# 21 of 44 gate and up tile pairs by seven block products instead of eight

## The chip, the cores and the metric

The kernel runs on one core of a Trainium2 chip. The metric is the time of one execution on the device in microseconds; the kernel before has a median of 1558.62 over 3 runs (1556.32 to 1564.79). The engines are TensorE (PE, products, with its weight loads shown apart as PEld), VectorE (DVE), ScalarE (ACT), GpSimd (POOL) and SyncE (SP, which here only issues DMAs).

## The reference

Two layers on x of 512 positions by 1024. Each layer normalises and modulates x, runs a retention branch and a causal pooling branch, merges them with sigmoid gates, projects, and adds the result to x. Then it normalises again to h2 and runs the feed-forward network (FFN):

```python
mod = c_act @ w_ada[l] + b_ada[l]
sh1, sc1, g1, sh2, sc2, g2 = jnp.split(mod, N_MOD, axis=-1)
...
h2 = modulate(rmsnorm(x, norm2[l]), sh2, sc2)
gate, up = jnp.split(h2 @ w_ffn_in[l], 2, axis=-1)
x = x + g2[:, None, :] * ((jax.nn.silu(gate) * up) @ w_ffn_out[l])
```

`w_ffn_in` is 1024 x 5632, so gate and up have 2816 columns each: 22 tiles of 128. The two layers have 44 pairs of a gate tile and the up tile of the same columns. All data are float32.

## The kernel before

Activations lie transposed: 128 channels on the partitions, 512 positions along a row. To keep float32 accuracy, both operands of a product are split in a high part, rounded to the type that TensorE multiplies fast, and a low part, the rest. `mm3` then makes three products: high weights by high activations, low by high, high by low. `project` runs `mm3` over all 128-channel blocks of the input into one PSUM bank of 128 x 512; there are eight banks (`ps`). An FFN tile has 8 blocks, so 24 products, and a pair 48.

Weights are packed in the order of use into chunks of eight 128 x 128 blocks (`wst`, 512 KB each). `prep` (L464) loads a chunk into a `raw` tile (SP's queue), casts it to `whi` and makes `wlo`: from chunk 16 on ACT writes minus `whi` into `wlo`, and a DMA issued by POOL adds the chunk from memory to it. `unit` (L483) calls `prep` for the chunk in use and, by `LOOK`, for the two behind it. There are 4 `raw` tiles and 5 each of `whi` and `wlo`.

The modulation vector is made on DVE: `mod_tile` (L531) loads a tile of `wada` (512 KB) into a `raw` tile too, and multiplies and sums it with the conditioning vector. `background` hands these out along the program: one per step of the gate loop behind retention, two per step of the pool loop, one per pair in the first FFN half and two in the second. Every `raw` tile, of `wst` or `wada`, is given out in the order in which it is asked for.

The FFN of a layer has two halves of 11 pairs. `first_tiles` (L615) makes the first three tiles, half a row (256 positions) at a time, while the second half of h2 is still being made. Behind each half `close` (L628) multiplies by `w_ffn_out` and adds to x.

The program is recorded first, and `Recorder.order` (L247) then sets the order of each engine by a list of costs: it follows time, gives each engine the operation that can start first or is due first, and lets some operations go to either of two engines (`either`: DVE or POOL; `copy`: ACT or DVE). Buffers of a kind are handed out in order of first use, except for temporaries and rows. PE's own order is that of the program. The engines then run their lists in order, held only by semaphores. As all operations are issued from one line, L390 in the profile is the line of every one of them.

## Time and profile before

| | us |
|---|---|
| median of 3 runs | 1558.62 |
| profiled execution | 1558.66 |
| its span, first to last instruction | 1556.9 |
| PE busy (x7302) | 1525.8 |
| ACT busy (x979) | 777.9 |
| DVE busy (x1133) | 642.7 |
| POOL busy (x331) | 299.8 |
| mean DMA rate | 212 GB/s |

The page shows busy time per engine over the span. A product's busy time overlaps with the next one's, so the pace of products is read from how many start in a stretch, not from the mean of one. A window row of a stretch has its length, the busy time (and instructions) of PE, PEld, DVE, ACT and POOL, the granted clock, the share of the DMA engines' time and the rate in GB/s. Layer 0's FFN runs from about 424 to 788 us (its first products of 256 columns with h2, its last with `w_ffn_out`), layer 1's from about 1182 to 1546.

### The profile page before, as it was taken

Reading aid. Unit: us, or ns where it says so; the run is one execution under the profiler, and the core shown is the slowest. Engines: PE = TensorE matmul, PEld = TensorE weight load, DVE = VectorE, ACT = ScalarE, POOL = GpSimd, SP = SyncE. Lnnn points to the kernel's source line nnn. Section 1 sums busy time; section 2 is a strip of 40 time slices with the busy share of each in tenths; the row PEclk is TensorE's granted clock in tenths of the full one; section 3 lists DMA queues with packets and bytes.
Section 4 is the critical chain, followed back from the end, with each engine's and each line's share of the span. In section 5 each row is a group of like instructions: output and inputs, shape, how many; then the busy total and the mean of one; then the engine's idle time right before and its main releaser. Section 6 shows DMA issues by size and latency. Waiting matters only on the chain.

```text
span 1556.9 us, 18913 instructions
## 1 busy us (share of the span) xinstructions
PE 1525.8 (98%) x7302; PEld 1272.8 (82%) x7302; DVE 642.7 (41%) x1133; ACT 777.9 (50%) x979; POOL 299.8 (19%) x331
## 2 busy tenths in 40 slices
PE   7899999999999999999999999999999999999997
PEld 6688878788988888888897888888889888888887
DVE  8977681245453212233265647314346111011123
ACT  3376664444554433444377777445346443344442
POOL 3212241111111111311111212211111111111110
PEclk9999999999999999999999999999999999999999
DMA  7766859999789999999789686999997998988972
GB/s 256 249 195 150 220 132 237 250 253 290 182 224 256 250 202 240 289 268 269 150 197 233 149 181 144 233 243 261 244 266 165 215 190 191 196 192 191 190 152 77
DMA packets 94589, 329.68 MB, mean 212 GB/s; under 512 B 10529, under 2 KB 12833, under 8 KB 94498
## 3 DMA queue, kind: packets, MB, share of 16 engines
q0 software_dynamic: 35280, 128.47, 47.4%
q1 hardware_dynamic: 59218, 200.00, 37.6%
q8 instruction: 57, 0.93, 0.2%
q14 instruction: 34, 0.28, 0.1%
HBM read 326.32 MB, written 2.10 MB: 211 GB/s over the span
## 4 chain that ended last, share of the span: by engine, by line
PE 91%; DVE 5%; DMA 2%; ACT 1%; issue 1%; POOL 0%; DVEq 0%; SPq 0%; ACTq 0%
PE ps L390 91%; DVE t L390 1%; DVE raw L390 1%; DMA wlo<-wst 1%; DVE mod L390 1%; DMA raw<-wst 1%; DVE r L390 0%; DMA xall<-xT 0%; ACT whi L390 0%; ACT t L390 0%; DVE h L390 0%; ACT r L390 0%; POOL wlo L390 0%; DVE s L390 0%; DVE wlo L390 0%
## 5 line engine op out<-in xcount | busy, mean ns | idle before, releaser
L390 PE MATMUL ps<-h,whi 128*128 128x512 f32 (+1 forms) x2720 | 804.0, 379 | 8.1 <-DVE h L390 5.6
L390 PEld LDWEIGHTS ps<-h,whi 128*128 128x128 f32 x2720 | 499.2, 188 | 111.5 <-issue 4.1
L390 ACT CAST whi<-raw 128x1024 fp32r<-128x1024 f32 (+1 forms) x227 | 238.3, 1050 | 551.7 <-PE ps L390 428.4
L390 PE MATMUL ps<-h,wlo 128*128 128x512 f32 (+1 forms) x1360 | 506.6, 380 | 0.7 <-DMA wlo<-wst 0.7
L390 PE MATMUL ps<-r,whi 128*128 128x512 f32 (+1 forms) x1620 | 440.4, 356 | 3.8 <-DVE r L390 3.8
L390 POOL DMA_DIRECT2D wlo<-wst x245 | 214.1, 874 | 1075.4 <-ACT wlo L390 923.0
L390 PEld LDWEIGHTS ps<-r,whi 128*128 128x128 f32 x1620 | 286.2, 188 | 53.4 <-DVE r L390 7.0
L390 PEld LDWEIGHTS ps<-h,wlo 128*128 128x128 f32 x1360 | 254.9, 188 | 47.4 <-DMA wlo<-wst 0.9
L390 PE MATMUL ps<-r,wlo 128*128 128x512 f32 (+1 forms) x810 | 289.0, 357 | 0.0
L390 ACT ACTIVATE wlo<-whi 128x1024 fp32r<-128x1024 f32 x245 | 259.6, 1061 | 19.0 <-DVE whi L390 11.5
L390 DVE SCALAR_TENSOR_TENSOR raw<-raw,cact 128x1024 f32<-128x1024 f32 x96 | 119.7, 1250 | 335.3 <-DMA raw<-wada 259.3
L390 PEld LDWEIGHTS ps<-r,wlo 128*128 128x128 f32 x810 | 152.2, 188 | 21.4
L390 DVE SCALAR_TENSOR_TENSOR xall<-ps,mod,xall 128x512 f32<-128x512 f32 (+1 forms) x62 | 38.9, 630 | 202.4 <-PE ps L390 202.4
L390 DVE TENSOR_TENSOR t<-ps,t 128x512 f32<-128x512 f32 x60 | 41.3, 689 | 194.8 <-PE ps L390 190.6
L390 PE MATMUL ps<-whi,h 128*128 128x512 f32 x256 | 80.6, 396 | 0.8 <-ACT r L390 0.8
L390 DVE TENSOR_TENSOR r<-t,r 128x512 fp32r<-128x512 f32 (+1 forms) x76 | 54.9, 722 | 9.9 <-ACT r L390 7.4
L390 PEld LDWEIGHTS ps<-whi,h 128*128 128x128 f32 x256 | 48.0, 188 | 12.7 <-ACT r L390 1.2
L390 ACT ACTIVATE t<-ps 128x512 f32<-128x512 f32 x76 | 44.5, 588 | 19.3 <-PE ps L390 19.1
L390 ACT COPY t<-ps 32x512 f32<-32x512 f32 (+1 forms) x72 | 41.5, 579 | 22.5 <-DVE t L390 11.0
L390 ACT ACTIVATE sq<-xall 128x256 f32<-128x256 f32 (+1 forms) x42 | 20.3, 486 | 63.6 <-DVE xall L390 63.3
L390 PE MATMUL ps<-wlo,h 128*128 128x512 f32 x128 | 50.6, 396 | 0.0
L390 ACT CAST r<-t 64x512 fp32r<-64x512 f32 (+1 forms) x60 | 36.9, 618 | 24.8 <-DVE t L390 22.9
(91 smaller groups left out, 868.3 us busy)
## 6 DMA issues: line engine op xcount, KB each, us to landing
raw<-wst SPq DMA_DIRECT2D x261, 512.0 KB, 4.8
wlo<-wst POOLq DMA_DIRECT2D x245, 512.0 KB, 7.1
raw<-wada SPq DMA_DIRECT2D x96, 512.0 KB, 6.5
tab<-rot SPq DMA_DIRECT2D x32, 256.0 KB, 4.8
xall<-xT SPq DMA_DIRECT2D x4, 512.0 KB, 6.5
out<-t SPq DMA_DIRECT2D x7, 256.0 KB, 2.4
out<-t SPq DMA_DIRECT2D x2, 128.0 KB, 2.3
tri<-trid SPq DMA_DIRECT2D x1, 128.0 KB, 5.0
```

The costliest lines, as they stand in the source:

```text
L390: getattr(eng, method)(*[real(a) for a in args], **{k: real(v) for k, v in kw.items()})
```

## The change

21 pairs, the even ones from 4 to 20 in layer 0 and in layer 1 those from 4 to 20 that 3 doesn't divide, are made by `seven`. It takes the 1024 input channels and the two output tiles (gate, up) as a 2 x 2 grid of weight blocks, and h2 as a 2 x 2 grid of channels by positions, each half a row long. A 2 x 2 product of blocks needs eight block products; with sums of blocks on either side (Strassen's method in Winograd's form) seven suffice, and the outputs are sums of the seven. In the code a seven has two chunks, each with the four weight blocks for two of the eight channel blocks: 2 chunks x 7 x 2 x 3 products of 256 columns, where a pair had 48 of 512.

What it adds around the products: `seven_prep` makes four sums of weight blocks per chunk (DVE), splits three of the four blocks themselves (768 columns) and all four sums, and no longer uses the accumulating DMA for them, so a seven's chunk fills four weight tiles, not two. Once per layer `make_h` also writes h2 unsplit (`whole`), and four sums per channel pair are made of it and split. Behind the products one copy (ACT) and five sums (DVE) put gate and up together from four PSUM banks.

SBUF is laid out anew: 3 `raw` tiles for 4; one set of 11 weight tiles `w` for the 10 of `whi` and `wlo`; 8 double tiles `x` for the rotary tables, the scores and `q_low`, and for the sums of h2. The squares go to the temporaries. `background` gives two tiles per step in the gate loop (one before), one per plain pair and per output tile of the first half's `close`, and none at a seven. A change of ACT's function table now counts as part of an operation's cost when the order is made. Two chunks are added for alignment.

```diff
-HALF_FT = FT // 2
+FF_CUTS = (0, 11, FT)
...
-N_CHUNKS = -(-N_UNITS // UNITS)
+N_CHUNKS = -(-N_UNITS // UNITS) + DEPTH
...
-N_RAW, N_SPLIT, N_H, N_ROW, N_TEMP, N_SCORE, N_SQ = 4, 5, 2 * KT, 28, 9, 5, 2
+N_RAW, N_W, N_X, N_H, N_ROW, N_TEMP = 3, 11, 8, 2 * KT, 28, 9
...
+SEVEN = [set(range(4, FT, 2)), {i for i in range(3, FT) if i % 3}]
+HALF_KT = KT // 2
...
                     if e == "scalar" and o.table is not None and o.table != table:
-                        t = max(t, free[e] + TABLE_US)
+                        d += TABLE_US
...
-    def raw_tile(dt=F32):
-        return nc.tile(wp, [P, UNITS * P], dt, "raw", N_RAW)
+    def weights():
+        return nc.tile(wp, [P, UNITS * P], F32R, "w", N_W)
+
+    def raw_tile():
+        return nc.tile(wp, [P, UNITS * P], F32, "raw", N_RAW)
+
+    def pair_tile(dt=F32):
+        return nc.tile(ap, [P, 2, S], dt, "x", N_X)
...
     def prep(c, n=1):
-        if c >= N_CHUNKS or c in his:
+        if c >= N_CHUNKS or c in his or c in sevens:
             return
-        raw = raw_tile()
+        raw, hi, lo = raw_tile(), weights(), weights()
         nc.sync.dma_start(out=raw, in_=wst[c])
-        hi = nc.tile(wp, [P, UNITS * P], F32R, "whi", N_SPLIT)
-        lo = nc.tile(wp, [P, UNITS * P], F32R, "wlo", N_SPLIT)
-        if c >= FIRST_ADDED:
+        if FIRST_ADDED <= c:
 
...
+    sevens = {}
+
+    def seven_chunk(l, i, k0):
+        c = len(order) // UNITS
+        assert len(order) % UNITS == 0
+        for k, col in ((0, 0), (HALF_KT, 0), (HALF_KT, FF), (0, FF)):
+            for d in range(2):
+                order[(l, "ffn_in", k + k0 + d, col + i * P)] = len(order)
+        sevens[c] = None
+        return c
+
+    def seven_prep(c):
+
+        if sevens[c] is not None:
+            return
+        w = 2 * P
+        af = raw_tile()
+        nc.sync.dma_start(out=af, in_=wst[c])
+        ah, al, sh, sl = (weights() for _ in range(4))
+        a11, a12, a22, a21 = (af[:, n * w:n * w + w] for n in range(4))
+        s34, s21 = keep(F32), keep(F32)
+        nc.vector.tensor_sub(out=s34[:, :w], in0=a21, in1=a11)
+        nc.vector.tensor_add(out=s21[:, :w], in0=s34[:, :w], in1=a22)
+        nc.vector.tensor_add(out=s21[:, w:], in0=a21, in1=a22)
+        nc.vector.tensor_sub(out=s34[:, w:], in0=a12, in1=s21[:, :w])
+        copy(ah[:, :3 * w], af[:, :3 * w])
+        if ADD_SEVEN:
+            nc.scalar.activation(al[:, :3 * w], ah[:, :3 * w].bitcast(F32), AF.Copy, scale=-1.0)
+            nc.gpsimd.dma_start(out=al[:, :3 * w], in_=wst[c][:, :3 * w], accum_op=ALU.add)
+        else:
+            nc.either.tensor_sub(out=al[:, :3 * w], in0=af[:, :3 * w], in1=ah[:, :3 * w].bitcast(F32))
+        for n, sf in enumerate((s34, s21)):
+            part = slice(n * S, n * S + S)
+            copy(sh[:, part], sf)
+            nc.either.tensor_sub(out=sl[:, part], in0=sf, in1=sh[:, part].bitcast(F32))
+        sevens[c] = (ah, al), (sh, sl)
...
-        for cc in range(c, c + look[0] + 1):
-            prep(cc)
+        ahead(c)
         sl = slice(o * P, (o + n) * P)
         return his[c][:, sl], los[c][:, sl]
+
+    def ahead(c):
+        for cc in range(c, c + look[0] + 1):
+            if cc in sevens:
+                seven_prep(cc)
+            else:
+                prep(cc)
...
+        if whole is not None:
+            nc.add({
+                "scalar": ("activation", (whole, t, AF.Identity), dict(bias=sh)),
+                "vector": ("tensor_scalar", (), dict(out=whole, in0=t, scalar1=sh, scalar2=None, op0=ALU.add)),
+            })
...
             m_.append(m)
-            background()
+            background(2)
...
+        whole = [(keep(F32), keep(F32)) for _ in range(HALF_KT)]
+        sums = [(pair_tile(F32R), pair_tile(F32R)) for _ in range(HALF_KT)]
...
+        while len(order) % UNITS:
+            order[("none", len(order))] = len(order)
+        done = first_tiles(l, 2, h2, "ffn_in", [0, FF, P], norm_b, block)
+        for k in range(HALF_KT):
+            t13, t24 = temp(), temp()
+            b11, b21, b12, b22 = (block(kk, n) for n, kk in ((0, k), (0, k + HALF_KT), (1, k), (1, k + HALF_KT)))
+            nc.either.tensor_sub(out=t13[:, A], in0=b12, in1=b11)
+            nc.either.tensor_sub(out=t13[:, B], in0=b12, in1=b22)
+            nc.either.tensor_sub(out=t24[:, A], in0=b22, in1=t13[:, A])
+            nc.either.tensor_sub(out=t24[:, B], in0=b21, in1=t24[:, A])
+            hi, lo = sums[k]
+            for n, t in enumerate((t13, t24)):
+                copy(hi[:, n], t)
+                nc.either.tensor_sub(out=lo[:, n], in0=t, in1=hi[:, n].bitcast(F32))
+
+        def seven(i):
+
+            cs = [seven_chunk(l, i, k0) for k0 in (0, 2)]
+            o = [ps() for _ in range(4)]
+            for k in range(HALF_KT):
+                ahead(cs[k // 2])
+                if k % 2:
+                    continue
+                (ah, al), (sh, sl) = sevens[cs[k // 2]]
+
+                for (wh, wl), n, bank, at, act in (
+                    ((ah, al), 0, 0, 0, "b11"), ((ah, al), 1, 1, 0, "b21"), ((ah, al), 2, 3, 1, 3),
+                    ((sh, sl), 2, 1, 1, 2), ((sh, sl), 3, 2, 0, 0), ((sh, sl), 0, 2, 1, 1), ((sh, sl), 1, 3, 0, "b22"),
+                ):
+                    for d in range(2):
+                        ws = slice((2 * n + d) * P, (2 * n + d + 1) * P)
+                        if isinstance(act, str):
+                            a = hs(h2[k + d + HALF_KT * (act[1] == "2")], A if act[2] == "1" else B)
+                        else:
+                            a = tuple(z[:, act // 2, act % 2 * 256:act % 2 * 256 + 256] for z in sums[k + d])
+                        first = k + d == 0 and (bank, at) in ((0, 0), (1, 0), (3, 1), (2, 0))
+                        last = k + d == HALF_KT - 1 and (bank, at) in ((0, 0), (1, 1), (2, 1), (3, 0))
+                        mm3(o[bank][:, at * 256:at * 256 + 256], (wh[:, ws], wl[:, ws]), a, first, last)
+            m1 = temp()[:, A]
+            nc.scalar.copy(out=m1, in_=o[0][:, A])
+            gate, up, u = temp(), temp(), temp()
+            nc.vector.tensor_add(out=gate.halves(), in0=o[1].halves(), in1=m1.twice())
+            nc.vector.tensor_add(out=u.halves(), in0=o[2].halves(), in1=gate[:, B].twice())
+            nc.vector.tensor_add(out=gate[:, B], in0=u[:, A], in1=o[3][:, A])
+            nc.vector.tensor_add(out=up[:, A], in0=u[:, B], in1=o[3][:, B])
+            nc.vector.tensor_add(out=up[:, B], in0=u[:, B], in1=o[2][:, A])
+            nc.scalar.activation(gate, gate, AF.Silu)
+            nc.either.tensor_mul(out=gate, in0=gate, in1=up)
+            return split(gate)
+        for f, (i0, i1) in enumerate(zip(FF_CUTS, FF_CUTS[1:])):
             hid = []
-            for i in range(f * HALF_FT, (f + 1) * HALF_FT):
+            for i in range(i0, i1):
+                if i in SEVEN[l]:
+                    hid.append(seven(i))
+                    continue
                 gu = []
                 for c in (i * P, FF + i * P):
                     if done:
...
                 nc.scalar.activation(sg, gu[0], AF.Silu)
                 nc.vector.tensor_mul(out=sg, in0=gu[1], in1=sg)
                 hid.append(split(sg))
-                background(1 + f)
+                background()
```

In the orders below L390 is the issuing line of the kernel before and L409 that of the changed one; `_` and a number tell buffers apart.

On PE, inside the second FFN half of layer 0: before, the end of one tile and the start of the next (`h` is h2, `whi` and `wlo` the split weights).

```order
L390 MATMUL ps_5515<-h_3667,whi_5383 128x512
L390 MATMUL ps_5515<-h_3667,wlo_5390 128x512
L390 MATMUL ps_5515<-h_3677,whi_5383 128x512
L390 MATMUL ps_5557<-h_3551,whi_5383 128x512
L390 MATMUL ps_5557<-h_3551,wlo_5390 128x512
L390 MATMUL ps_5557<-h_3562,whi_5383 128x512
```

Now, inside a seven (`x` are the sums of h2, `w` the split weights or sums of weights).

```order
L409 MATMUL ps_5853<-h_3589,w_5714 128x256
L409 MATMUL ps_5853<-h_3592,w_5714 128x256
L409 MATMUL ps_5853<-h_3592,w_5722 128x256
L409 MATMUL ps_5853<-h_3605,w_5714 128x256
L409 MATMUL ps_5864<-x_3829,w_5714 128x256
L409 MATMUL ps_5864<-x_3829,w_5722 128x256
L409 MATMUL ps_5864<-x_3840,w_5714 128x256
L409 MATMUL ps_5864<-x_3882,w_5714 128x256
L409 MATMUL ps_5864<-x_3882,w_5722 128x256
L409 MATMUL ps_5864<-x_3915,w_5714 128x256
L409 MATMUL ps_5853<-x_3829,w_5745 128x256
L409 MATMUL ps_5853<-x_3829,w_5751 128x256
```

A tile went into one bank with 512 columns each; now a product takes half a row, the banks alternate within a chunk, and each group of six reads another block of weights.

On DVE, the same part of the program. Before, what one pair asks of it (the product with silu, a split, and two `wada` tiles):

```order
L390 TENSOR_TENSOR t_5403<-ps_5401,t_5403 128x512
L390 CAST r_5447<-t_5403 128x512
L390 TENSOR_TENSOR r_5451<-t_5403,r_5447 128x512
L390 SCALAR_TENSOR_TENSOR raw_5429,mod_0_4216<-raw_5429,cact_73 128x1024
L390 SCALAR_TENSOR_TENSOR raw_5478,mod_0_4216<-raw_5478,cact_73 128x1024
```

Now, from a plain pair to a seven (`raw_6118` is the chunk of a seven, `raw_6049` is read by a cast alone):

```order
L409 CAST w_6148<-raw_6049 128x1024
L409 TENSOR_TENSOR r_6162<-raw_6118 128x256
L409 CAST w_6170<-raw_6118 128x768
L409 TENSOR_TENSOR w_6178<-raw_6118,w_6170 128x768
L409 TENSOR_TENSOR r_6190<-r_6162,raw_6118 128x256
L409 TENSOR_TENSOR r_6190<-raw_6118 128x256
L409 CAST w_6201<-r_6190 128x512
L409 TENSOR_TENSOR w_6207<-r_6190,w_6201 128x512
L409 TENSOR_TENSOR r_6162<-raw_6118,r_6190 128x256
L409 TENSOR_TENSOR t_6217<-ps_6081,t_6154 128x512
L409 TENSOR_TENSOR w_6207<-r_6162,w_6201 128x512
L409 TENSOR_TENSOR w_6229<-raw_6151,w_6209 128x768
```

A chunk that DVE did not touch before now takes up to ten of its instructions in a row. `w_6148`, the cast of `raw_6049`, is read by no product: in the whole program 42 chunks of sevens are first cast, negated and added to in the plain way, with that outcome.

On SP's queue, the loads of about two pairs. Before:

```order
L390 DMA raw_5235<-wst 128x1024
L390 DMA raw_5249<-wada 128x1024
L390 DMA raw_5272<-wada 128x1024
L390 DMA raw_5286<-wst 128x1024
L390 DMA raw_5311<-wst 128x1024
L390 DMA raw_5324<-wada 128x1024
```

Now (`raw_6034` and `raw_6049` are the plain loads of the two chunks that `raw_6118` and `raw_6151` load again; `raw_5992` and `raw_6181` belong to a plain pair):

```order
L409 DMA raw_5992<-wst 128x1024
L409 DMA raw_6034<-wst 128x1024
L409 DMA raw_6049<-wst 128x1024
L409 DMA raw_6085<-wada 128x1024
L409 DMA raw_6118<-wst 128x1024
L409 DMA raw_6151<-wst 128x1024
L409 DMA raw_6181<-wst 128x1024
```

Two chunks and two `wada` tiles per pair became, for a seven and a plain pair together, six loads of chunks and one of `wada`, through three tiles. Over the program there are 305 loads of `wst` on this queue, 261 before, and 247 accumulating loads on POOL's, 245 before.

65 lines of the change are left out of this document (45 added, 20 removed).

## The prediction

> **What bounds the kernel now.** I read the page's engine line and chain of waits first, then the stages, then the pace of single products. The columns of a stage are its length, then busy time and number of instructions of each engine, granted clock, DMA share and rate.
>
> ```profile
> span 1556.9 us, 18913 instructions
> PE 1525.8 (98%) x7302; PEld 1272.8 (82%) x7302; DVE 642.7 (41%) x1133; ACT 777.9 (50%) x979; POOL 299.8 (19%) x331
> ...
> PE 91%; DVE 5%; DMA 2%; ACT 1%; issue 1%; POOL 0%; DVEq 0%; SPq 0%; ACTq 0%
> ```
>
> ```profile
> 0.00:73.00 73.00, 58.38 (x254) 46.42 (x254) 66.04 (x106) 24.00 (x31) 23.48 (x21) 0.95 0.78 254
> ...
> 434.00:600.00 166.00, 166.00 (x757) 137.52 (x756) 44.84 (x77) 73.74 (x78) 26.88 (x31) 1.00 0.94 234
> 600.00:794.00 194.00, 194.00 (x967) 164.31 (x966) 63.05 (x118) 87.08 (x98) 38.57 (x40) 1.00 0.94 242
> ...
> 1154.00:1310.00 156.00, 156.00 (x847) 135.14 (x846) 48.02 (x96) 73.92 (x93) 24.29 (x28) 1.00 0.87 194
> 1310.00:1540.00 230.00, 230.00 (x1076) 191.78 (x1075) 37.42 (x60) 93.23 (x104) 33.79 (x39) 1.00 0.82 171
> ```
>
> The last four rows cover the FFN of the two layers, where the change lies, and some work at its edges. TensorE (PE) is busy in all 746 us of them; the others have room, though the DMA share stands at 0.82 to 0.94. So here a product less is time less, as long as what feeds TensorE stays ahead of it.
>
> **The products.** A plain pair makes 2 tiles x 8 blocks x 3 products of 512 columns: 48. A seven makes 2 x 7 x 2 x 3 = 84 of 256 columns. The pace of each kind, from stretches of one kind alone:
>
> ```profile
> 1310.00:1480.00 170.00, 170.00 (x744) 139.51 (x743) 24.57 (x39) 70.11 (x73) 26.88 (x31) 1.00 0.90 192
> ...
> 400.00:420.00 20.00, 20.00 (x170) 19.95 (x170) 7.47 (x15) 8.78 (x13) 2.56 (x3) 1.00 0.45 98
> ...
> 424.00:439.00 15.00, 15.00 (x125) 14.78 (x124) 14.78 (x37) 9.51 (x19) 0.89 (x1) 1.00 0.58 147
> ```
>
> 170/744 = 0.2285 us for 512 columns; 20/170 = 0.1176 for 256, more than half (0.1142), because there the weight loads (PEld) are 19.95 of 20 us busy: they set the pace. A pair is 48 x 0.2285 = 10.97 us, a seven 84 x 0.1176 = 9.88: 1.09 us gained, x 21 = **22.8 us**, not the eighth (28.8) that the column count gives. The third row shows that pace held (0.12) with the vector engine (DVE) 99% busy, so I charge nothing for the sums' traffic beside the loads.
>
> The Trainium skill speaks against the change here: "TensorE: Matmul & The Clock Gate", section "Back-to-back issue gap", gives about 81 ns for a product of 128 columns and 131 for 512 in a stream of loads and products. An estimate from that page, in a straight line between them, is 98 ns for 256, so 84 x 0.098 = 8.2 against 48 x 0.131 = 6.3: each seven 1.9 us longer, about 41 us in all. The trace has 228 and 118 ns, so the sum goes by the trace; what the page would make of it here is the last rival below.
>
> **What feeds them: a preparation made twice.** Looking ahead from a plain tile, `prep` reaches a seven's chunk before `seven_chunk` has entered it in `sevens`, so it is prepared as a plain chunk too, and nothing reads that. The order shows 42 such chunks: 305 loads of `raw` for 261, and 247 accumulating loads for 245, where 42 should have gone. Each seven still pays 4 plain loads and 2 accumulating ones. The price is in the DMA queues' view, first of the page (packets, MB, share of 16 engines), then of 605 to 720 us (issues, KB, us to landing):
>
> ```profile
> q0 software_dynamic: 35280, 128.47, 47.4%
> q1 hardware_dynamic: 59218, 200.00, 37.6%
> ```
>
> ```profile
> 605.00:720.00 115.00, 115.00 (x505) 94.33 (x504) 38.91 (x68) 48.86 (x51) 26.43 (x26) 1.00 1.01 271
> ...
> raw<-wst SPq DMA_DIRECT2D x22, 512.0 KB, 5.9
> wlo<-wst POOLq DMA_DIRECT2D x21, 512.0 KB, 7.3
> raw<-wada SPq DMA_DIRECT2D x18, 512.0 KB, 7.3
> ```
>
> Layer 0 alternates seven and plain: 20.85 us of TensorE with 7 plain and 4 accumulating loads, 0.336 and 0.192 per us. Layer 1 has two sevens to a plain pair: 30.73 us with 10 and 6, 0.325 and 0.195. The stretch quoted carried 40 and 21 in 115 us, 0.348 and 0.183, with TensorE never idle. So the amount of DMA is known ground.
>
> New is that `raw` has three tiles, not four. A tile's turn is its landing (5.9 us, 7.3 for `wada`) and its reading. Readings, from the groups by shape (after the bar: busy us, mean ns):
>
> ```profile
> L390 ACT CAST whi<-raw 128x1024 fp32r<-128x1024 f32 x226 | 237.7, 1052 | 551.7 <-PE ps L390 428.4 <-DMA raw<-wst 123.2
> ...
> L390 DVE SCALAR_TENSOR_TENSOR raw<-raw,cact 128x1024 f32<-128x1024 f32 x96 | 119.7, 1250 | 335.3 <-DMA raw<-wada 259.3 <-issue 32.3 <-ACT whi L390 31.9
> ...
> L390 DVE TENSOR_TENSOR r<-t,r 128x512 fp32r<-128x512 f32 x60 | 41.5, 692 | 2.0
> ...
> L390 DVE CAST r<-t 128x512 fp32r<-128x512 f32 x64 | 27.5, 430 | 2.2
> ...
> L390 DVE CAST whi<-raw 128x1024 fp32r<-128x1024 f32 x34 | 23.6, 695 | 29.8 <-PE ps L390 25.2 <-DMA raw<-wst 4.0 <-POOL r L390 0.4
> ...
> L390 ACT ACTIVATE h<-t,mod 128x256 fp32r<-128x256 f32 x44 | 21.8, 506 | 15.0 <-DVE t L390 14.9
> ...
> L390 DVE TENSOR_TENSOR acc<-acc,sq 128x256 f32<-128x256 f32 x27 | 11.7, 433 | 11.1 <-ACT sq L390 11.1
> ...
> L390 DVE TENSOR_TENSOR wlo<-raw,whi 128x1024 fp32r<-128x1024 f32 x7 | 8.4, 1223 | 0.7 <-ACT whi L390 0.5
> ```
>
> A seven's chunk is read by four sums of 256 (0.433 each), a cast and a difference of 768 (halfway between the rows of 512 and 1024: 0.56 and 0.96): 3.25 us on DVE. A plain or wasted one is read by a cast (1.05), a `wada` one in 1.25. Layer 0: (6 x 5.9 + 7.3 + 2 x 3.25 + 4 x 1.05 + 1.25)/3 = 18.2 us for a period of 20.85. Layer 1: (10 x 5.9 + 4 x 3.25 + 6 x 1.05)/3 = 26.1 for 30.73. They hold, with 13 to 15% to spare, if a landed tile waits on average no more than 1.1 us (layer 0) or 1.4 us (layer 1) for its reader.
>
> That reader is mostly DVE, which takes its instructions in order. The 32 DVE rows of a period of layer 0's second half, priced by these groups (8 sums and 3 output sums of 256 at 0.433, 10 of 512 at 0.69, 3 casts of 1024, 1 of 768 and 4 of 512, 2 differences of 768, one `wada`), come to 19.2 us of 20.85, 92%; 134 rows over six sevens and three plain pairs of layer 1 come to 78 of 92 us. Before, layer 0's first FFN half gave DVE 45 of 166 us (434 to 600). So DVE becomes nearly as full as TensorE. It also takes 181 casts of whole chunks, not 34, and such a cast waits until TensorE frees a weight tile; behind it stand the output sums that free PSUM banks. A seven holds four of the eight banks, so TensorE has a pair's length, some 10 us, before it waits for those. What that costs is not shown for 350 us on end (9 sevens and 8 pairs, 12 and 5), but two short stretches are like it:
>
> ```profile
> 420.00:434.00 14.00, 13.85 (x110) 13.22 (x109) 13.46 (x35) 9.20 (x18) 1.75 (x2) 1.00 0.92 231
> ...
> 786.00:796.00 10.00, 10.00 (x85) 9.87 (x83) 9.26 (x25) 6.29 (x12) 1.72 (x2) 1.00 1.03 268
> ```
>
> ```profile
> 796.80 0.38 PE L390 MATMUL ps<-h,wlo 128*128 128x256 f32 x1 [0.67 <-DMA wlo<-wst]
> ```
>
> With DVE over 92% and the DMA full, TensorE lost 0.15 us in 420 to 439 and 0.67 right after 796: 0.82 of 30 us, 2.7%. On 350 us that is **9.5 us** lost. The ends are 0 (as in 605 to 720) and the 30 us of the second rival below.
>
> **The rest.** Retention's gate loop now asks for two `wada` tiles per step instead of one, and the pool loop keeps two, on three `raw` tiles. A step of the pool loop has 36 products, 8.23 us, and 1.5 chunks: (1.5 x 6.95 + 2 x 8.55)/3 = 9.2 us for `raw` (6.9 with four). Eight steps of layer 0 would lack 7.6 us, and layer 1 asks for only 11 tiles there; the chunks prepared ahead (11 weight tiles, five chunks of 5.5 us each) cover most. I take **2 us** (0 to 8). The 16 extra whole-precision copies of `h` per layer and the blocks' sums lie under three plain pairs: nothing (16 x 0.5 us on ACT, bare). The start could go either way: DVE loses its stops behind POOL's differences, and the weights' `raw` tile has to land, be cast and be subtracted in a row.
>
> ```profile
> 21.71 2.94 POOL L390 TENSOR_TENSOR wlo<-raw,whi 128x1024 fp32r<-128x1024 f32 x1 [18.06 <-ACT whi L390]
> ```
>
> ```profile
> 22.35 2.31 DVE L390 TENSOR_TENSOR mod<-mod,vec 128x1 f32<-128x1 f32 x1
> ...
> 28.91 2.32 DVE L390 TENSOR_TENSOR mod<-mod,vec 128x1 f32<-128x1 f32 x1
> ```
>
> ```profile
> raw<-wst SPq DMA_DIRECT2D x7, 512.0 KB, 4.4
> ```
>
> A step now takes 6.6 us (28.91 - 22.35), 2.3 of it a one-column sum held up while POOL subtracts; with the difference on DVE (1.22) it would be some 1.1 us shorter. The tile's own chain is 4.4 + 1.05 + 1.22 and a few semaphores, 6.9 us. Seven steps: -7 to +2; I take 0, by the chain.
>
> Sum: the profiled execution took 1558.7 us (span 1556.9 and 1.8 around it; the median is 1558.62, the same). 1558.7 - 22.8 + 9.5 + 2 = **1547 us**.
>
> **Rivals.** *Nothing is lost*: the waits fall into the spare 13%, as in 605 to 720. 1558.7 - 22.8 = 1536. For it: DMA load and pace have both been seen. Against: DVE was a third busy then.
>
> *The raw tiles run dry behind DVE*: a landed tile waits behind an earlier seven's output, 2 sums of 512, 3 of 256, a product and a difference, 4.1 us by their rows, half of that on average: 2 us. Layer 0's period becomes (54.7 + 14)/3 = 22.9, layer 1's (78.3 + 20)/3 = 32.8: 2.05 x 9 + 2.05 x 6 = 30 us lost, 1558.7 - 22.8 + 30 + 2 = 1568, slower. It decides from 1.1 us of waiting on, and each further microsecond costs some 40.
>
> *The DMA engines are the bound*: by the queues' rows an accumulating load takes 0.474 x 1557/245 = 3.0 us of all 16 engines, a plain one (0.524 MB) 0.376 x 1557 x 0.524/200 = 1.53. Layer 0 needs 22.8 of 20.85 us, layer 1 33.4 of 30.73: 17 + 16 us, 1571. Against: 605 to 720 asked for 124 of 115 us and got it. The Trainium skill, "Perfetto Trace Analysis", section "Identifying the Most-Contended Engine", calls the occupancy of the 16 engines misleading; the trace agrees, with a share of 1.00 at 281 GB/s and 1.01 at 271.
>
> ```profile
> 340.00:380.00 40.00, 40.00 (x176) 32.81 (x176) 21.34 (x37) 15.16 (x18) 6.08 (x7) 1.00 1.00 281
> ```
>
> *Loads outgrow the half products*: above 0.1306 us (10.97/84) a seven loses outright; at 0.14, 21 x (11.76 - 10.97) = 17 us, 1575. The 99% stretch speaks against it.
>
> **How the numbers follow.** The forecast has 0.50, nothing lost 0.18, dry tiles 0.22, full DMA 0.05, loads 0.02, the unnamed 0.03. A half per cent, about what can be told apart here, is 7.8 us: 1550.8 to 1566.4. Nothing lost and 0.39 of the forecast lie below, 0.57. The forecast's upper 0.11 and some 0.09 of the dry tiles lie between, 0.20. The rest, 0.23, is slower. The forecast's own range is 1538 to 1560. For 8 in 10 I reach from below the full gain (a start some 3 us better) to beyond the dry tiles: 1533 to 1574.
>
> **What would show it.** In the profile after: 84 products of 256 columns per seven at 0.118 us; TensorE idle in the four FFN stretches of some 10 us in all, in short gaps released by DVE or by a DMA into `w`; DVE at 80 to 90% there; 305 loads of `raw`. Wrong would be: gaps before each seven (dry tiles), a pace over 0.13, or a start or pool loop that moved by more than 8 us.

## The result and the profile after

The changed kernel takes 1632.8 us (median of 4 runs, 1629.0 to 1639.4), the kernel before 1557.5 beside it: a ratio of **1.048** (95% interval 1.043 to 1.053). It is slower by 75 us; I had said 1547, faster by 11, with a range up to 1574.

First lines of the page, and the shares of the chain of waits by engine and by line:

```profile
span 1637.6 us, 21319 instructions
PE 1536.2 (94%) x8058; PEld 1314.2 (80%) x8058; DVE 980.3 (60%) x1748; ACT 700.5 (43%) x983; POOL 337.1 (21%) x370
...
PE 43%; DMA 33%; DVE 11%; issue 8%; ACT 3%; POOL 1%; DVEq 0%; SPq 0%; ACTq 0%; POOLq 0%
PE ps L409 43%; DMA raw<-wada 13%; DMA w<-wst 10%; DMA raw<-wst 9%; DVE w L409 4%; DVE t L409 3%; ACT w L409 2%; DVE raw L409 2%; DVE r L409 1%; POOL w L409 1%; ACT t L409 1%; DMA xall<-xT 0%; POOL r L409 0%; DVE x L409 0%; DVE h L409 0%
```

Before, 91% of the chain was TensorE and 2% DMA; now a third is landings. TensorE stands idle for 101.4 us (1637.6 - 1536.2), 31.1 before. And its busy time, which should have fallen by 22.8 to 1503, rose by 10: the granted clock of the execution is 0.969, 0.995 before. No engine is full.

The stages, cut at the first product of V and of the FFN and at the last output product of the FFN in each layer (length; busy time and instructions of PE, PEld, DVE, ACT, POOL; clock; DMA share; GB/s). First before: attention of layer 0, its FFN, the hand-over, attention and FFN of layer 1.

```profile
73.03:423.04 350.01, 346.40 (x1630) 286.31 (x1630) 185.98 (x310) 199.12 (x275) 77.23 (x87) 1.00 0.82 211
423.04:788.52 365.48, 365.46 (x1761) 306.92 (x1762) 113.48 (x208) 163.29 (x181) 65.47 (x71) 1.00 0.93 238
788.52:812.18 23.66, 22.99 (x170) 21.74 (x170) 17.05 (x39) 15.96 (x26) 4.44 (x5) 1.00 0.77 184
812.18:1181.81 369.63, 366.72 (x1727) 304.56 (x1726) 178.04 (x320) 215.57 (x280) 72.27 (x82) 1.00 0.85 213
1181.81:1546.53 364.72, 364.72 (x1762) 306.56 (x1761) 77.50 (x140) 157.88 (x186) 56.92 (x66) 1.00 0.83 178
```

The same of the changed kernel:

```profile
71.35:433.58 362.23, 348.26 (x1632) 288.77 (x1630) 216.66 (x372) 167.18 (x238) 84.13 (x89) 0.98 0.82 216
433.58:834.32 400.74, 372.07 (x2087) 324.56 (x2086) 232.20 (x427) 149.91 (x205) 76.31 (x85) 0.95 0.86 230
834.32:861.10 26.78, 24.58 (x171) 23.19 (x170) 18.47 (x41) 15.13 (x27) 3.49 (x4) 0.94 0.80 197
861.10:1235.20 374.10, 368.26 (x1728) 306.75 (x1726) 213.72 (x368) 174.19 (x243) 78.86 (x86) 0.99 0.84 212
1235.20:1627.34 392.14, 362.78 (x2194) 323.59 (x2193) 236.11 (x415) 170.66 (x241) 91.38 (x92) 0.97 0.81 203
```

The two FFN stages, which should have become 9.8 and 13.1 us shorter, are 35.3 and 27.4 longer: some 86 us went there against the sum of products. The three other stages lost 12.2, 3.1 and 4.5; the start gained 1.7.

What TensorE waits for, in the view of waits (us in total, times, longest):

```profile
PE ps L409 <- DMA w<-wst: 53.5, 15, 8.8
PE ps L409 <- DVE r L409: 18.0, 6, 8.5
```

The second row is mostly the products right behind retention's gate loop, told below. The first is the FFN: of its fifteen waits twelve, 50 of the 53.5 us, stand before the *plain* pair behind a seven, the other three (3.3 us) elsewhere; a seven's weights need no accumulating load. Before, the whole program had 0.7 us of such waits, on this line of the page:

```profile
L390 PE MATMUL ps<-h,wlo 128*128 128x512 f32 (+1 forms) x1360 | 506.6, 380 | 0.7 <-DMA wlo<-wst 0.7
```

The longest after, at 1478 us, shows how it comes about. In the order of the four fences: ScalarE, GpSimd, TensorE in the timeline, then a piece of the chain of waits.

```profile
1459.08 1.29 ACT L409 CAST w<-r 128x512 fp32r<-128x512 f32 x2
1466.54 1.06 ACT L409 CAST w<-raw 128x1024 fp32r<-128x1024 f32 x1 [6.17 <-DMA w<-wst]
1467.63 2.01 ACT L409 ACTIVATE w<-w 128x1024 fp32r<-128x1024 f32 x2
```

```profile
1469.05 1.82 POOL L409 DMA_DIRECT2D w<-wst  x2 [9.61 <-ACT w L409]
```

```profile
1478.22 7.07 PE L409 MATMUL ps<-h,w 128*128 128x512 f32 x23 [8.78 <-DMA w<-wst]
```

```profile
1469.05 9.13 DMA w<-wst
```

ScalarE has a chunk to cast and stands for 6.17 us until an accumulating load has landed *in the tile it is to write*. Products release a weight tile by having read it; this one was the low part of a chunk prepared for nobody, and is free only when its own load has landed. Behind the standing cast are the copies with the sign turned, behind these GpSimd's issue of the next accumulating loads, 9.61 us idle; these take 9.13 to land, and TensorE stands 8.78 before its plain pair.

Then the clock, around the gap that ends at 736.75 us. First TensorE's timeline, then stretches of time (columns as for the stages):

```profile
736.75 13.50 PE L409 MATMUL ps<-h,w 128*128 128x512 f32 x52 [4.89 <-DMA w<-wst]
```

```profile
725.00:731.00 6.00, 6.00 (x54) 6.00 (x53) 5.79 (x12) 2.56 (x4) 0.88 (x1) 1.00 0.62 189
731.00:736.70 5.70, 0.85 (x7) 0.53 (x5) 2.63 (x5) 2.46 (x4) 1.73 (x2) 0.77 0.98 250
736.70:739.00 2.30, 2.25 (x5) 1.84 (x6) 0.00 (x0) 0.40 (x1) 0.86 (x1) 0.50 1.05 240
739.00:741.00 2.00, 2.00 (x6) 1.57 (x5) 1.53 (x3) 0.00 (x0) 0.00 (x0) 0.54 1.04 281
741.00:743.00 2.00, 2.00 (x10) 1.62 (x9) 1.79 (x5) 0.00 (x0) 0.00 (x0) 1.00 1.03 258
```

After 4.89 us of standing, TensorE runs at half clock until 740.85, for 4.1 us (11 products in 4.3 us, where some 19 fit at the full clock): this gap costs about 2 us more than its length. That is how the busy time rose.

### The profile page after: what moved, and what is told of

It reads as the page before. It is cut to its first block, busy times and chain, and to the rows that moved or that the text cites. A ratio compares the mean times of both kernels' runs of the same rounds, so it can differ in the third digit from the quotient of the medians.

```text
span 1637.6 us, 21319 instructions
## 1 busy us (share of the span) xinstructions
PE 1536.2 (94%) x8058; PEld 1314.2 (80%) x8058; DVE 980.3 (60%) x1748; ACT 700.5 (43%) x983; POOL 337.1 (21%) x370
## 4 chain that ended last, share of the span: by engine, by line
PE 43%; DMA 33%; DVE 11%; issue 8%; ACT 3%; POOL 1%; DVEq 0%; SPq 0%; ACTq 0%; POOLq 0%
PE ps L409 43%; DMA raw<-wada 13%; DMA w<-wst 10%; DMA raw<-wst 9%; DVE w L409 4%; DVE t L409 3%; ACT w L409 2%; DVE raw L409 2%; DVE r L409 1%; POOL w L409 1%; ACT t L409 1%; DMA xall<-xT 0%; POOL r L409 0%; DVE x L409 0%; DVE h L409 0%
## 5 line engine op out<-in xcount | busy, mean ns | idle before, releaser
L409 PE MATMUL ps<-h,w 128*128 128x512 f32 (+1 forms) x3828 | 791.9, 365 | 59.1 <-DMA w<-wst 51.3
L409 PEld LDWEIGHTS ps<-h,w 128*128 128x128 f32 x3828 | 655.9, 194 | 178.7 <-DMA w<-wst 56.0
L409 PE MATMUL ps<-r,w 128*128 128x512 f32 (+1 forms) x2430 | 484.5, 359 | 19.9 <-DVE r L409 17.6
L409 PEld LDWEIGHTS ps<-r,w 128*128 128x128 f32 x2430 | 405.1, 189 | 93.0 <-DVE r L409 20.9
L409 ACT ACTIVATE w<-w 128x1024 fp32r<-128x1024 f32 x247 | 260.3, 1058 | 426.3 <-DVE w L409 158.1
L409 POOL DMA_DIRECT2D w<-wst x247 | 220.3, 895 | 1052.4 <-ACT w L409 909.2
L409 DVE CAST w<-raw 128x1024 fp32r<-128x1024 f32 (+2 forms) x202 | 140.1, 693 | 200.7 <-DMA raw<-wst 134.1
L409 DVE SCALAR_TENSOR_TENSOR raw<-raw,cact 128x1024 f32<-128x1024 f32 x96 | 120.5, 1258 | 166.8 <-DMA raw<-wada 163.1
L409 ACT CAST w<-raw 128x1024 fp32r<-128x1024 f32 (+2 forms) x104 | 103.6, 997 | 161.8 <-DMA raw<-wst 126.7
L409 PE MATMUL ps<-x,w 128*128 128x256 f32 x1008 | 125.1, 279 | 1.0 <-ACT t L409 1.0
L409 PEld LDWEIGHTS ps<-x,w 128*128 128x128 f32 x1008 | 121.1, 188 | 1.2 <-ACT t L409 1.2
L409 PE MATMUL ps<-w,h 128*128 128x512 f32 x384 | 90.2, 395 | 0.0
L409 PEld LDWEIGHTS ps<-w,h 128*128 128x128 f32 x384 | 72.1, 188 | 17.5
L409 DVE TENSOR_TENSOR w<-raw,w 128x768 fp32r<-128x768 f32 (+2 forms) x55 | 64.4, 1172 | 24.7 <-DMA w<-wst 12.2
L409 DVE SCALAR_TENSOR_TENSOR xall<-ps,mod,xall 128x512 f32<-128x512 f32 (+1 forms) x62 | 38.8, 628 | 65.7 <-PE ps L409 65.6
L409 ACT CAST r<-t 128x512 fp32r<-128x512 f32 (+1 forms) x97 | 59.6, 617 | 34.4 <-DVE t L409 27.0
L409 DVE TENSOR_TENSOR w<-r,w 128x512 fp32r<-128x512 f32 x81 | 54.4, 688 | 24.8 <-ACT w L409 16.1
L409 DVE TENSOR_TENSOR t<-ps,t 128x512 f32<-128x512 f32 x81 | 55.3, 683 | 15.3 <-PE ps L409 13.2
L409 ACT CAST w<-r 128x512 fp32r<-128x512 f32 x55 | 32.5, 617 | 71.9 <-DVE r L409 40.7
L409 DVE TENSOR_TENSOR r<-raw 128x256 f32<-128x256 f32 x84 | 41.3, 514 | 35.1 <-DMA raw<-wst 34.9
L409 DVE TENSOR_TENSOR r<-t,r 128x512 fp32r<-128x512 f32 (+1 forms) x78 | 56.7, 727 | 7.4 <-ACT r L409 6.2
L409 ACT COPY t<-ps 32x512 f32<-32x512 f32 (+2 forms) x93 | 48.8, 527 | 18.9 <-DVE t L409 11.2
```

The source lines that it names most:

```text
L409: getattr(eng, method)(*[real(a) for a in args], **{k: real(v) for k, v in kw.items()})
```

## The experiments

Eighteen kernels, in five groups. Where nothing else is said, an edit is one to the changed kernel, and a number is the median; stage lengths are those of the one profiled execution. Times can be compared with 1632.8 (the change) and 1557 to 1561 (before, beside each group).

### What the loss hangs on

*One preparation per chunk* (the sevens' chunks and the plain ones get their places in `order` before the loop looks ahead):

```
+        chunks = {}
+        for k in range(KT):
+            for c in (0, FF, P):
+                order[(l, "ffn_in", k, c)] = len(order)
...
+                if i in SEVEN[l]:
+                    chunks[i] = [seven_chunk(l, i, k0) for k0 in (0, 2)]
+                    continue
...
-            cs = [seven_chunk(l, i, k0) for k0 in (0, 2)]
+            cs = chunks[i]
```

> The changed kernel (1632.8 us) with one thing mended: the chunks of the sevens are given their places before anything looks ahead, so none of the 42 is prepared a second time as a plain chunk that nothing reads (261 raw loads instead of 305, some 205 accumulating loads instead of 247). Products, tiles and the rest of the change stay. Theory 1 (the double preparation starves the plain pair behind a seven): the loss inside the two FFN stages, 37 and 33 us by the landmarks of the two traces, mostly goes: 1632.8 - 60 = 1573, and 1560 to 1590 would bear it out; the idle time ahead of plain pairs released by a DMA into a weight tile falls from 53 us to under 15. Theory 2 (three raw tiles and the new layout cost it anywhere): only the loads that are gone count; 1610 to 1630. Theory 3 (the order planned with landings of 3.5 and 6.2 us where 6 to 9 are needed): less waste lets landings fall, a part goes; 1590 to 1615.

Measured **1553.5**, ratio to before 0.996 (0.994 to 0.998): 79 us came back, more than theory 1 asked for. The FFN stages are now shorter than before, by 6.0 and 11.5 us; attention and hand-over stay long (362.9, 26.6, 373.7):

```profile
433.97:793.42 359.45, 357.23 (x2087) 316.11 (x2086) 220.46 (x393) 139.15 (x196) 73.09 (x74) 1.00 0.76 205
1193.63:1546.87 353.24, 351.89 (x2194) 317.03 (x2193) 226.56 (x385) 142.03 (x213) 83.63 (x78) 1.00 0.61 154
640.00:723.40 83.40, 83.40 (x529) 75.55 (x528) 56.16 (x99) 29.61 (x41) 14.22 (x16) 1.00 0.65 178
```

*No sevens, all else of the change:*

```
-SEVEN = [set(range(4, FT, 2)), {i for i in range(3, FT) if i % 3}]
+SEVEN = [set(), set()]
```

> The changed kernel without any seven: all 44 pairs by eight products of blocks, as before, with everything else of the change (three raw tiles, the pools laid out anew, two background chunks per gate step, the planner's new charge for a table load; the sums of h2 are still made and not read). No chunk is prepared twice here. Theory 2: what the layout costs stays, all of the 26 us lost outside of the FFN and some in it: 1585 to 1600. Theory 1: outside of the FFN the losses (12 us in layer 0's attention, 11 and 5 in layer 1's) are not of the sevens, inside nothing is lost: 1575 to 1590. If the sevens alone cost everything, downstream stages too (their weights being late), it is 1555 to 1565.

Measured 1600.0, 1.024 (1.018 to 1.030), at the upper end of theory 2's range. So 40 us hang here on what is not the sevens; in the profiled execution, the slowest of the four at 1606.8, 14.5 are in layer 0's attention, 20.6 in its FFN, 12.7 in hand-over and layer 1's attention, 2.0 in its FFN. The parts do not add up over kernels: the FFN of plain pairs alone loses more on this layout than that with sevens prepared once. A plain pair asks for two accumulating loads, a seven for none; whether that is why was not tried.

*The old rule for table loads* in the planner (as before the change, `t = max(t, free[e] + TABLE_US)`):

> The changed kernel with the planner's old rule for table loads (a table load delays the start and is not charged to the instruction's cost), so that whole-chunk casts go back to ScalarE (34 of them were on VectorE before, 181 after). Theory 4 (VectorE is overfilled by that rule, and the outputs of the sevens behind such casts are late): 1632.8 falls by 20 to 50 us, 1580 to 1610, and busy time of DVE by some 100 us (980 to 880). Theories 1 and 3: within 10 us of 1632.8.

Measured 1637.8, 1.048 (1.044 to 1.053): nothing. DVE still has 182 whole-chunk casts, so the rule is not what put them there; theory 4 is out.

*Longer landings in the planner:*

```
-LANDS = 5.0
-LATENCY = {"tensor": 0.19, "vector": 0.05, "scalar": 0.05, "gpsimd": 0.05, "sync": 1.6}
+LANDS = 7.5
+LATENCY = {"tensor": 0.19, "vector": 0.05, "scalar": 0.05, "gpsimd": 0.05, "sync": 4.0}
```

> The changed kernel with the planner told of longer landings: 7.5 us instead of 5.0 after the issue of an accumulating load, 4.0 instead of 1.6 for a plain one, about what the trace shows in the FFN (8 to 9.6 and 6 to 7.4 from issue). Nothing else differs; only the order of the instructions and the places of those that may go to either engine. Theory 3 (the order is at fault): the gaps ahead of plain pairs shrink, 1632.8 falls by 20 to 50 us, 1580 to 1610. Theory 1 and 2: the loads are still as many on three raw tiles, 1620 to 1645.

Measured 1585.8, 1.016 (1.011 to 1.021): 47 us back with the double preparation still there. Theory 3 holds beside theory 1. With single preparation the same edit is worth only 12 us (1541.2 for 1553.5, below), so some 35 of the 47 hang on both together: loads that nobody needs, and an order that counts on early landings.

### Which part of the second preparation

Three kernels take parts of it away (`TWICE` lists the 42 chunks), a fourth narrows its accumulating load.

```
-            nc.gpsimd.dma_start(out=lo, in_=wst[c], accum_op=ALU.add)
+            if c not in TWICE:
+                nc.gpsimd.dma_start(out=lo, in_=wst[c], accum_op=ALU.add)
```

> The changed kernel (1632.8 us) in which the 42 chunks prepared a second time still take their raw tile, their load, their cast and their copy with the sign turned, and two weight tiles, but are not followed by the accumulating load (205 of these instead of 247). Nothing reads what they hold. The first runs showed that the whole second preparation is worth 79 us (1553.5 without it). Theory A (the accumulating loads hold the DMA engines and the weight tiles 8 to 9 us each): most of it goes, 1560 to 1580. Theory B (the raw tiles: three of them, and 42 more turns): 1615 to 1635. Theory C (it is the sum of both, landings growing with all that is under way): about half, 1585 to 1605.

Measured 1581.2: 51 back, between the ranges of theories A and C.

```
-        raw, hi, lo = raw_tile(), weights(), weights()
-        nc.sync.dma_start(out=raw, in_=wst[c])
+        hi, lo = weights(), weights()
+        if c in TWICE:
+            raw = cact
+        else:
+            raw = raw_tile()
+            nc.sync.dma_start(out=raw, in_=wst[c])
```

> The counterpart: the 42 second preparations take no raw tile and no load into it; their cast reads a tile that is there for good (of the same shape), the copy with the sign turned and the accumulating load go out as in the change, and the two weight tiles are held. Nothing reads what they hold. Theory A (accumulating loads): 1615 to 1635, as the changed kernel. Theory B (raw tiles run dry): most of the 79 us goes, 1560 to 1580. Theory C (both): 1585 to 1605.

Measured 1600.5 (three executions within 1 us of it, the fourth at 1580.9): 32 back, theory C. Both kinds cost, and 51 and 32 make 83, where the whole second preparation is worth 79. This edit takes away a turn of a `raw` tile and the traffic of its load at once; which of the two the 32 us are is not told apart.

Both edits at once, so that only casts and negated copies are left:

> The changed kernel in which the 42 second preparations do neither of their loads: the cast (from a tile that is there for good) and the copy with the sign turned are issued as in the change, and the two weight tiles are held for these two instructions. Nothing reads them. Without any second preparation it is 1553.5 us. If the loads are the whole cost: 1550 to 1560. If the casts in VectorE's order and the weight tiles have a cost of their own: 1565 to 1585.

Measured 1555.7, 77 back, within the noise of single preparation (1553.5): the casts and copies cost nothing that shows. It is the loads, with what they hold until they land.

```
-            nc.gpsimd.dma_start(out=lo, in_=wst[c], accum_op=ALU.add)
+            w = P if c in TWICE else UNITS * P
+            nc.gpsimd.dma_start(out=lo[:, :w], in_=wst[c][:, :w], accum_op=ALU.add)
```

> The changed kernel with all second preparations whole but for one thing: the accumulating load of each of the 42 moves one eighth (64 KB of 512). It is still issued from POOL in its place and its weight tile is still held until it has landed; nothing reads that tile. Taking these loads away altogether was worth 51 us (1632.8 to 1581.2). If it is their traffic that costs (the landings of the loads beside them): 1580 to 1600. If it is the place they take in POOL's and ScalarE's order and the weight tiles they hold: 1615 to 1635.

Measured 1603.5, between the two ranges: 29 of the 51 are gone with seven eighths of the bytes, 22 stay with the load's presence. In this trace every engine takes the instructions of the changed kernel in the same order, so the 29 us come from the bytes. Taking loads away, as in the three kernels above, also lets the planner place later instructions anew. An eighth of the bytes lands hardly sooner (issues: count, KB, us to landing):

```profile
w<-wst POOLq DMA_DIRECT2D x205, 512.0 KB, 8.0
...
w<-wst POOLq DMA_DIRECT2D x42, 64.0 KB, 6.8
```

### By which way

In the view of waits of the changed kernel, the engines that write weight tiles stand, in order, before a tile that is still being filled:

```profile
ACT w L409 <- DMA w<-wst: 49.0, 12, 9.6
...
DVE w L409 <- DMA w<-wst: 20.8, 11, 4.5
...
POOL w L409 <- DMA w<-wst: 13.5, 2, 7.3
```

83 us in all; with single preparation the view has one such wait:

```profile
DVE w L409 <- DMA w<-wst: 0.5, 1, 0.5
```

The next edit changes no load and no tile: the planner alone takes the landing of those 42 loads as 4 us later.

```
             lands = LANDS if e == "gpsimd" and o.forms[e][0] == "dma_start" else 0.0
+            lands += 4.0 * getattr(o, "unread", False)
...
             nc.gpsimd.dma_start(out=lo, in_=wst[c], accum_op=ALU.add)
+            nc.ops[-1].unread = c in TWICE
```

> The changed kernel, in which the planner takes the landing of the 42 accumulating loads that nothing reads for 9 us instead of 5, and so hands their weight tiles on 4 us later; the loads, the tiles and all other assumptions are the same. Standing time of ScalarE, VectorE and GpSimd before a weight tile that is still being filled: 83 us now, expected under 40. If this standing, in engines that take their instructions in order, is a way by which the second preparation delays TensorE: 1632.8 falls by 15 to 30, 1603 to 1618. If it is the loads' traffic and the raw tiles alone: 1625 to 1640.

Measured **1610.5**, 22 less, with 37 us of such standing:

```profile
ACT w L411 <- DMA w<-wst: 17.4, 7, 5.5
POOL w L411 <- DMA w<-wst: 13.7, 2, 7.0
DVE w L411 <- DMA w<-wst: 6.3, 4, 2.1
```

So this way is real: in the profiled execution the two FFN stages are 12.7 and 9.5 us shorter. It is also of the size of the 22 us that stayed with the narrow loads; that they are the same 22 us is not shown. Then plain loads' landing alone (`"sync": 4.0`):

> The changed kernel, in which the planner takes 4.0 us instead of 1.6 from a plain load's issue to its landing, with nothing changed for accumulating loads. Together with 7.5 us for these it gave 1585.8, 47 less. If late raw tiles, behind which VectorE and ScalarE stand 296 us in all, are the larger part: 1590 to 1610, with the attention of layer 0 back at some 350 us. If the accumulating loads' landing was the larger part: 1612 to 1635.

Measured 1607.7, 25 less, of which the profiled execution has 15.4 in layer 0's attention (362.2 to 346.8). The 22 and the 25 add up to the 47 of both landings set right together, but they are not its two parts: there all accumulating loads were counted 2.5 us later, here 42 of them 4 us. The edit of `LANDS` alone was not run.

*One weight tile more* (twelve, in the room of two temporaries), and *a fourth raw tile for the eleventh weight tile:*

```
-N_RAW, N_W, N_X, N_H, N_ROW, N_TEMP = 3, 11, 8, 2 * KT, 28, 9
+N_RAW, N_W, N_X, N_H, N_ROW, N_TEMP = 3, 12, 8, 2 * KT, 28, 7
```

> The changed kernel with twelve weight tiles instead of eleven, in the room of two small temporaries (seven instead of nine); double preparation and three raw tiles stay. If the weight tiles run out in the FFN (a seven's two chunks hold eight of them, the plain pair behind it needs four, and the two second preparations four more): the FFN stages fall by 10 to 15 us each, 1600 to 1615. If the tiles are not what is short, or the two temporaries are missed: 1625 to 1645.

```
+N_RAW, N_W, N_X, N_H, N_ROW, N_TEMP = 4, 10, 8, 2 * KT, 28, 9
```

> The changed kernel with four raw tiles and ten weight tiles instead of three and eleven, the double preparation left in. Theory 2 (raw tiles): attention back by 13 to 15 us in layer 0 and 4 to 5 in layer 1, and, since 42 raw turns less were worth 32 us in the FFN, some 20 to 30 there: 1580 to 1600. If a weight tile less costs as much as a raw tile brings (a seven's chunk holds four of them, a chunk prepared twice two that nothing needs): 1625 to 1650.

Measured 1629.7 and 1624.5: neither number of tiles mends it. Twelve weight tiles bring the standing before a filling tile down to 37 us, but ScalarE's standing before raw tiles goes from 127 to 281. Four raw tiles shorten layer 0's attention by 10.7 us, and the missing weight tile raises the other standing to 127.5. Both expectations that put a number of tiles at fault fell.

### Outside of the FFN

*The kernel before with three raw tiles instead of four* (`N_RAW` alone), and *the change without sevens with four raw and ten weight tiles:*

> The kernel before with three raw tiles instead of four, nothing else (no seven, no new pools, no change of the planner). Four raw tiles in the changed kernel without sevens brought 21 us back, 15 of them in layer 0's attention. Theory 2 (the third raw tile too few is the loss outside of the FFN): 1575 to 1590, layer 0's attention 12 to 15 us longer than its 350.0. If three tiles hurt only with the new pools, with two wada chunks per step of the gate loop: 1557 to 1566.

> The changed kernel without sevens (1600.0 us, 40 over the kernel before) with four raw tiles and ten weight tiles instead of three and eleven, as the kernel before had four and ten. Theory 2 (three raw tiles cost what the new layout loses): 1560 to 1572. If it is the second wada chunk of each step of the gate loop, or the planner's charge for tables, or that weights' halves now share one set of tiles: 1590 to 1603.

Measured 1574.3 (1.010, 1.006 to 1.013) and 1578.8 (1.011, 1.006 to 1.015). Three raw tiles cost the kernel before 14 us, just under the expected range; its profiled execution, 20 us longer than the one before, has 9.6 of them in layer 0's attention, 5.2 in its FFN, 6.3 in layer 1's attention. Four bring the changed kernel without sevens 21 back, between the two expected ranges, with the attention at 349.3 and 368.9 (350.0 and 369.6 before). So in that kernel the raw tile explains the attention. Some 18 us remain in that kernel, 14.6 in layer 0's FFN, where TensorE stands 7.8 us at the first output product; what else of the layout they come from was not tried.

One profile settles little about a stage. In the changed kernel and in seven others, all with three raw tiles (no sevens, single preparation, the four with parts of the second preparation taken away or narrowed, the later landing of the 42 loads), the engines take the same instructions in the same order until after 450 us, yet layer 0's attention took from 354.6 to 364.5 us. The 349.3 with four raw tiles and the 346.8 with later plain landings lie outside of that; a difference of less than 10 us in one stage says little by itself.

### A version that beats both

> Both things that made the changed kernel faster at once: every chunk prepared once (1553.5 us alone) and the planner told of landings of 7.5 and 4.0 us (1585.8 alone). By the landmarks of the two traces, layer 0's attention takes 349.9 us instead of 362.9 and layer 1's 368.5 instead of 373.7 with the longer landings, and the FFN 359.5 and 353.2 with single preparation: if the two add up, 1553.5 - 18 - 2 = 1533 (1525 to 1540). If the longer landings only hid the lateness which the second preparation made, nothing is left to hide in the FFN but the attention's part stays: also 1535 to 1545. If they work on one and the same loss, 1550 to 1556.

> Each chunk prepared once and the planner told of longer landings (1541.2 together), and four raw tiles and ten weight tiles. What is left to win by the landmarks of the run with three raw tiles: layer 0's attention 353.8 for 349.3, layer 1's 365.9 (nothing), the FFN 357.4 and 346.6 for the 355.7 and 351.6 of the predicted price (nothing): 1535 to 1540 if the raw tiles still bind. If one weight tile less starves the sevens: 1545 to 1560.

> Each chunk prepared once, the longer landings, and four raw tiles with eleven weight tiles, in the room of two temporaries. With three and eleven it is 1541.2, with four and ten 1538.4. If raw tiles bind the attention and weight tiles the FFN: 343.9 and 366 us of attention, 357 and 347 of FFN, some 1527 (1522 to 1533). If the temporaries are missed: 1540 to 1550.

> As before it, with twelve weight tiles and five temporaries. If weight tiles still bind at eleven: 1518 to 1526. If eleven are enough: within 3 us of the kernel with eleven. If five temporaries are too few: 1540 to 1560.

Single preparation and longer landings: **1541.2**, ratio to before 0.985 (0.981 to 0.990). With four raw and ten weight tiles 1538.4, 0.986 (0.984 to 0.989). Four raw and eleven weight tiles with seven temporaries, 1544.2, and twelve with five, 1540.2, missed what I had expected of them (1527, and 1518 to 1526): here a tile gained is a temporary lost. The first two and the last can't be told from one another; each of these three beats both kernels, the one before by 1.2 to 1.5%, the changed one by 5.6 to 5.8%.

## Why the prediction was wrong, step by step

**The pace and the products: right.** With single preparation a seven and a plain pair alternate undisturbed; of the products that only a seven has, the first 24 of each of four sevens start at:

```profile
649.64 2.99 PE L409 MATMUL ps<-x,w 128*128 128x256 f32 x24
...
670.52 2.99 PE L409 MATMUL ps<-x,w 128*128 128x256 f32 x24
...
691.40 2.99 PE L409 MATMUL ps<-x,w 128*128 128x256 f32 x24
...
712.28 2.99 PE L409 MATMUL ps<-x,w 128*128 128x256 f32 x24
```

20.88 us a period, 20.85 predicted. The 22.8 us are there: 17.5 arrive in the FFN stages of that kernel (6.0 + 11.5), so 5.3 are lost, where I had put 9.5. The rival of loads that outgrow half products is out.

**The preparation made twice, "known ground": the step that failed.** I had found the 42 chunks, and priced them by their amount: 0.35 plain and 0.18 accumulating loads per us had been carried before without a gap. That such a rate had been carried was right, and not the point. Before, TensorE waited 0.7 us in the whole program for an accumulating load, so how long one took mattered little. The low half of a wasted chunk is freed by the landing itself, and the next writer is placed by a planner that counts on 5 us after GpSimd's issue, where 8 to 9 pass from issue to landing. I reckoned the DMA's throughput and never asked what *releases* the weight tiles of a chunk that nothing reads, nor what the order takes for granted. The price is 79 us, of which 77 are the two kinds of loads. Shown of the 77 are 22 by the standing before such tiles (later hand-over, same loads) and 29 by the bytes of the accumulating loads (same order); how the plain loads' 32 divide between `raw` tiles and traffic stays open, and these parts may overlap.

With the sizes measured, my own sum closes: 1558.7 - 22.8 + 5.3 + 19.8 (the rest, below) + 79 = 1640 (the start's 1.7 us left aside), and the profiled execution took 1639.4.

**The raw tiles: in the forecast at no loss, and mis-sized.** I held that three tiles turn in 18.2 of 20.85 us, with the landing of 5.9 that the kernel before showed from 605 to 720 us. In the changed kernel's FFN, from 640 to 740 us, it is longer:

```profile
raw<-wst SPq DMA_DIRECT2D x25, 512.0 KB, 7.4
w<-wst POOLq DMA_DIRECT2D x17, 512.0 KB, 9.2
raw<-wada SPq DMA_DIRECT2D x4, 512.0 KB, 5.2
```

With 7.4 and 5.2 my own sum is (6 x 7.4 + 5.2 + 6.5 + 4.2 + 1.25)/3 = 20.5 us: all but 0.3 us of the spare is gone before a landed tile has waited for its reader. Taking the raw loads of the second preparation away was worth 32 us. That this is near the rival's 30 is in part luck: the rival had tiles wait for DVE's output sums, while here landings are longer, and the edit took traffic away too. The sign I had given for it was misplaced: I looked for gaps before each seven, but they stand before the plain pair, whose accumulating load comes last.

**DVE at 92%: wrong, and without effect.** A period of the second half of layer 0's FFN takes 14.0 us of DVE with single preparation (56.16 over four periods), 67%, and 16.5 in the changed kernel, not 19.2. The casts of the second preparation cost nothing that shows (only they and the copies left: 1555.7); what DVE's other whole-chunk casts cost was not tried. DVE matters as an engine that stands in order, not as one that is full.

**DMA engines as a steady bound: out.** Their share in the two FFN stages is 0.86 and 0.81, below the 0.93 and 0.83 of before, while TensorE starves, and later landings in the planner bring 47 us back with the same loads. Around the gap shown above the share is 0.98 to 1.05 (731 to 743 us), and narrower loads bring 29 back: for short stretches the traffic does count.

**The rest, 2 us (0 to 8): mis-sized.** Attention and hand-over of both layers lost 12.2 + 3.1 + 4.5 = 19.8 us. I had priced the pool loop and let the gate loop's second `wada` pass. The longest gap stands right behind the gate loop, at the products of the pooling groups; in the chain of waits and on TensorE:

```profile
295.90 9.67 DMA raw<-wada
...
306.93 3.67 DMA raw<-wst
```

```profile
312.06 3.35 PE L409 MATMUL ps<-r,w 128*128 128x512 f32 x7 [8.52 <-DVE r L409]
```

DVE stands for two landings in a row, the product that TensorE needs behind it. By the kernel before with three raw tiles, most of it is the raw tile; by the planner's landing for plain loads alone (layer 0's attention at 346.8), it is the order as much.

**What no term held: the clock.** I priced a gap at its length. The same 8058 products took 1536.2 us here and 1511.0 with single preparation: 25 of some 80 us between the two profiled executions are busy time, 55 are the gaps. The 25 are the clock: in the stretches at a granted 0.50 TensorE is busy for 77.0 us here and for 29.2 with single preparation, and half of that difference is 24.

**The start: right**, 1.7 us shorter within -7 to +2. Of the signs that I had named, the 305 loads came; TensorE stood 58 us in the two FFN stages, not some 10, mostly for DMAs into `w`, and DVE stayed at 58 and 60% there, not at 80 to 90. Of what would show me wrong, the nearest is layer 0's attention, which holds the pool loop and was 12.2 us longer.

## What to carry to other kernels

For work that is done for nothing, price what it holds and what frees it, not only what it moves: a buffer without a reader is freed by its own transfer, and the next writer stands, with all that is queued behind it on an engine that works in order. Where a written order rests on assumed landings, compare these with the medians of the stretch in question, under the load that the change will make, before believing any spare of 10 to 15%. And add to each expected gap on TensorE the stretch at half clock that can follow it.
